# A two-layer diffusion trunk: kernel tiles of the state space loaded during the gates, modulation two row blocks a step

## The chip, the cores and the metric

The kernel runs on one core of one Trainium2 chip. The metric is the device time of one execution in microseconds (us); the time of a kernel is the median of its runs.

## What is computed

Two trunk layers over 256 context tokens and 256 latent tokens of width 1024, all in float32. Each layer computes, for both streams (the second layer for the latent one only, beyond k, v and u of the context):

```
mods = silu(c) @ ada_w + ada_b                         # 6 x 1024 per stream: shift, scale, gate, twice
h    = rmsnorm(x) * (1 + scale) + shift
q, k, v, u, g = split(h @ w_in)
o    = differential attention (two softmax maps a head, 4 heads of 64, axial rotary)
y    = u * d + sum over both directions of C x,  x_t = lam_bar x_(t-1) + b_bar u_t     # 32 groups of 16 channels, 64 states
y    = gelu(y);  y = y * sigmoid(y @ w_glu + b_glu)
x    = x + gate1 * rmsnorm((sigmoid(ga) * (o' @ w_br_a) + sigmoid(gs) * (y @ w_br_s)) @ w_out)
x    = x + gate2 * rmsnorm(squared-ReLU MLP(rmsnorm(x) * (1 + scale2) + shift2))
```

## The kernel before

**Order of the work.** The Python program emits one straight line of instructions; the framework's scheduler (line 1419, with a simulated timeline) then orders the instructions of each engine by the place in the program and by when it thinks that operands and buffers are ready. So an instruction may run well before or after its place in the text. All DMAs but one kind go out on SP's queue in the order that results.

**Weights.** A weight unit is 128 x 1024 floats, 512 KB. prefetch (line 188) loads it into a raw tile, ACT copies it to whi, DVE (for some units POOL) subtracts to get wlo, and each product is three matmuls (mm3, lines 158 to 161). Raw tiles come from a pool of five buffers (RW), whi and wlo from four each.

**Modulation.** ada_gen (line 279) is a background task: for each of eight row blocks of ada_w it loads a raw tile (two for part 0), from the same five buffers, and runs four small matmuls into one PSUM bank ("ada"); then it evacuates. Parts 1 to 4 of each layer have eight blocks each. The bank has one buffer, which ssm_out also uses.

**Background.** pump (line 675) runs the next step of the first task in a list, up to its next yield. The counts of pumps at each place are tables: in layer 0 three after each k unit (PK) and each v tile (PV), none in gates 0 to 7, one in each later gate (PG); in layer 1 three after each k unit, none at q and v, one in each gate. In layer 0 the list holds ssm_in, ssm_out and then parts 1 to 4; two pumps (FE) of the last tail of layer 0 and then layer 1 take parts 1 to 4 of layer 1.

**State space.** The sequence is cut into 32 chunks of 8 tokens. Inside a chunk the output is a product with a local kernel: ssm_out (line 530) computes for each of four chunks of eight groups, c = 0 to 3, the rows of CL (chunk state to output, stored to cl, 1 MB) and the local kernel, stored to kd. M is the local kernel in shifted copies: each of 128 partitions reads rows of 128 floats, 16 floats further for each of 8 shifts, so that the DMA moves runs of 512 bytes. ygen (line 1035) loads two M tiles of 1 MB and CL, and computes y by blocks b of groups from U and M, and from the scanned states S2 and CL (line 1073). Part of CL goes to the small pool (CLl, NX quarters of 512 KB), the rest to large slots (CLs).

**Buffers.** slot gives one of 15 large buffers (8 KB a partition), which hold nearly everything; xtile gives one of three small buffers (4 KB a partition), which also serve as scratch of the SSM steps (cm) and as x of the tails.

**Around the y products.** After q, k and v come 16 gate units (lines 1110 to 1122) with the items of the attention and, in layer 1, the scan between them. s2copy (after gate 15 in layer 0, after gate 10 in layer 1) makes S2. The y tasks start after gate 15 (YA). Then come the pa units (attention output by gate), gelu, glu and psb.

Of the kernel before, what the change touches and what calls it, by code (L numbers as in the profile page):

```python
# [68 lines left out]
YA = [15, 15]  # L69
YN = [2, 1]  # L70
UA = {2: 1, 3: 3}
NX = [4, 2]
LW = [1, 0]
HFA = [(3,), (0, 1, 2, 3), (), (1, 2, 3)]
HFQ = [(), (0, 1, 2, 3)]
# [10 lines left out]
def trunk(tc, I, out):  # L86
    nc = tc.nc
    ctx = ExitStack()
    with ctx:
# [189 lines left out]
        def ada_gen(L, g):  # L279


            c0, n = (0, 512) if g == 0 else (1024 + 1024 * g, 256)
            ncb = n // 128
            ps = pd_.tile([128, 512], F32, name="ada")
            for k in range(8):
                rows = I["ada_w"][L, k * 128:(k + 1) * 128]
                if (L, g) == (0, 0) and k < AK:
                    full = slot([2, 1024], name="adaw")
                    S.dma_start(out=full.rearrange("p j c -> p (j c)"), in_=rows[:, 0:2048])
                    raws = [full[:, 0], full[:, 1]]  # L290
                else:
                    raws = []
                    for jp in range(n // 256):
                        raw = rawp.tile([128, 1024], F32, name="raw", tag="raw")
                        S.dma_start(out=raw, in_=rows[:, c0 + jp * 1024:c0 + (jp + 1) * 1024])
                        raws.append(raw)
                for j in range(4):
                    raw, o = raws[j * n // 1024], j * n % 1024
                    PE.matmul(ps[32 * j:32 * j + 32, :n], cs[:, k, :], raw[:, o:o + n], start=(k == 0), stop=(k == 7))  # L299
                yield  # L300
            R = m2(n, name="row")
            if g in (1, 4):
                ab, gr = m2(n, name="ab"), m2(n, name="gr")
                S.dma_start(out=ab, in_=I["adab"][L, :, g // 4])
                S.dma_start(out=gr, in_=I["grow"][L, :, g // 4])
                V.tensor_tensor(R, ps[:, :n], ab, op=OP.add)
                V.tensor_tensor(R, R, gr, op=OP.mult)
                dd = dram.tile([2, 1024], F32, name=f"ggd{L}_{g}")
                for j in range(4):
                    S.dma_start(out=dd[:, j * n:(j + 1) * n], in_=R[32 * j:32 * j + 2])  # L310
                ggd[L, g] = dd
            else:
                A.activation(R[:, 0:n // 2], ps[:, 0:n // 2], AF.Copy)
                V.tensor_copy(R[:, n // 2:n], ps[:, n // 2:n])
                for cb in range(ncb):
                    PE.transpose(ps[:, cb * 128:(cb + 1) * 128], R[:, cb * 128:(cb + 1) * 128], ident)
                mt = perl.tile([128, 4, ncb, 2], F32, name=f"mod{g}")
                ptv = ps[:, :n].rearrange("p (cb j w) -> p j cb w", cb=ncb, j=4)[:, :, :, 0:2]

                def col(o, nj):  # L320
                    return vecs[L][:, o:o + ncb * nj].rearrange("p (j c) -> p j c", j=nj)[
                        :, :, :, None].to_broadcast([128, nj, ncb, 2])
                V.tensor_tensor(mt, ptv, col({0: V_AB, 2: V_SH2, 3: V_SC2}[g], 4), op=OP.add)
                if g == 0:
                    V.scalar_tensor_tensor(mt[:, 2:4], mt[:, 2:4], 1.0, col(V_G0, 2), op0=OP.add, op1=OP.mult)
                elif g == 3:
                    V.scalar_tensor_tensor(mt, mt, 1.0, col(V_G2, 4), op0=OP.add, op1=OP.mult)
                mods[L, g] = mt.rearrange("p j cb v -> p (j cb) v")
            yield
# [9 lines left out]
        ssmt = {}  # L339

        def ssm_params(L):
# [123 lines left out]
            ssmt[L]["b2"] = pcs[:, 640:1696].rearrange("p (r g h) -> p r g h", r=2, g=33)  # L465
            ssmt[L]["et"] = [dram.tile([128, 8, 2, 128], F32, name=f"et{L}_{c}") for c in range(4)]
            ssmt[L]["cl"] = [dram.tile([128, 8, 2, 128], F32, name=f"cl{L}_{c}") for c in range(4)]
            ssmt[L]["kd"] = [dram.tile([16, 16, 240], F32, name=f"kd{L}_{h}") for h in range(2)]
            yield

        def ssm_b(L):
# [58 lines left out]
        def ssm_out(L, c):  # L530

            z = ssmt[L]
            cch = z["bc"][:, 2:4, 8 * c:8 * c + 8]
            C = slot([8, 2, 128], name="CL")
            Cv = C.rearrange("p g r (s h) -> p g r s h", s=8)
            cmul(L, c, Cv[:, :, 0], cch[:, 0], cch[:, 1], OP.subtract)
            yield
            cmul(L, c, Cv[:, :, 1], cch[:, 1], cch[:, 0], OP.add)
            S.dma_start(out=z["cl"][c], in_=C)
            yield  # L540
            pks = [tbank("kf"), pd_.tile([128, 512], F32, name="ada")]
            b2f = z["b2"].rearrange("p r g h -> p r (g h)")
            for g2, r, j, d in np.ndindex(2, 2, 4, 2):
                ro, gi = slice(64 * d, 64 * d + 64), 4 * g2 + j
                PE.matmul(pks[d][32 * j:32 * j + 32, g2 * 128:(g2 + 1) * 128],
                          b2f[ro, r, (8 * c + gi) * 16:(8 * c + gi) * 16 + 32], C[ro, gi, r, :],
                          start=(r == 0), stop=(r == 1), tile_position=(64 * d, 32 * j))
            kt = chk.tile([128, 2, 240], F32, name="kt")
            pf, pb_ = (p[:, 0:256].rearrange("p (g n) -> p g n", g=2) for p in pks)
            V.tensor_copy(kt[:, :, 0:128], pb_)  # L550
            V.tensor_tensor(kt[:, :, 112:128], kt[:, :, 112:128], pf[:, :, 0:16], op=OP.add)
            for g2 in range(2):
                o = V_D + 2 * c + g2
                V.scalar_tensor_tensor(kt[:, g2, 112:128], eye16, vecs[L][:, o:o + 1], kt[:, g2, 112:128],
                                       op0=OP.mult, op1=OP.add)
            V.tensor_copy(kt[:, :, 128:240], pf[:, :, 16:128])
            for j in range(4):
                o = 8 * (c % 2) + j
                S.dma_start(out=z["kd"][c // 2][:, o:o + 5:4], in_=kt[32 * j:32 * j + 16])
            z["done", c] = True  # L560
            yield

# [201 lines left out]
        for L in range(DEPTH):  # L764
# [266 lines left out]


            ysb, yg, ygh, ygl = [], [], [], []

            def ygen():
                ysb.append(slot([4 // A_, 8, 2, 64], name="ysb"))
                Ms = {}
                while ("done", 3) not in z:
                    pump()
                for gh in range(2):  # L1040
                    M = slot([16, 128], name="M")
                    kd = z["kd"][gh]
                    S.dma_start(out=M.rearrange("p g n -> p (g n)"),
                                in_=bass.AP(tensor=kd.tensor, offset=kd.offset, ap=[[16, 8], [240, 256], [1, 128]]))
                    Ms[gh] = M
                CLs = {}
                for qd in range(8):
                    if qd < NX[L]:
                        t = xtile("CLl").rearrange("p (g r n) -> p g r n", g=4, r=2)
                        S.dma_start(out=t, in_=z["cl"][qd // 2][:, qd % 2 * 4:qd % 2 * 4 + 4])  # L1050
                        CLs[qd] = t
                    elif qd % 2 or qd == NX[L]:
                        if qd % 2 == 0:
                            t = slot([8, 2, 128], name="CLs")
                            S.dma_start(out=t, in_=z["cl"][qd // 2])
                            CLs[qd], CLs[qd + 1] = t[:, 0:4], t[:, 4:8]
                        elif qd not in CLs:
                            t = slot([4, 2, 128], name="CLs")
                            S.dma_start(out=t, in_=z["cl"][qd // 2][:, 4:8])
                            CLs[qd] = t  # L1060
                    elif qd not in CLs:
                        t = slot([8, 2, 128], name="CLs")
                        S.dma_start(out=t, in_=z["cl"][qd // 2])
                        CLs[qd], CLs[qd + 1] = t[:, 0:4], t[:, 4:8]
                for b in range(8 // A_):
                    ps = bbank("y")
                    for gi, r, a in np.ndindex(4, 3, A_):
                        g = b * 4 * A_ + 4 * a + gi
                        if r == 0:
                            w, mv = U[:, g, 64 - ncol:64], Ms[g // 16][:, g % 16]  # L1070
                        else:
                            w, mv = S2[g // 16][:, g % 16, r - 1], CLs[g // 4][:, g % 4, r - 1]
                        PE.matmul(ps[ncol * a:ncol * a + ncol, gi * 128:gi * 128 + 128], w, mv,
                                  start=(r == 0), stop=(r == 2), tile_position=(0, ncol * a))
                    A.activation(ysb[0][:, b // 2, :, b % 2].rearrange("p t (g h) -> p g t h", g=4),
# [34 lines left out]
            for j in range(16):  # L1110
# [3 lines left out]
                step(at, -(-nitem * (j + 1) // AJ[L]) - -(-nitem * j // AJ[L]))  # L1114
                step(sc, 8)
                pump(PG[L][j // 4])
                if j == SJ[L]:
                    s2copy()
                if j >= YA[L]:
# [311 lines left out]
```

## Time and profile before

| | us |
|---|---|
| median of 3 runs | 1327.86 |
| lowest, highest | 1326.23, 1328.57 |
| the profiled execution | 1329.41 |
| its span, first to last instruction | 1327.3 |
| TensorE busy in it | 1236.9 (93%) |
| VectorE (DVE) busy | 876.1 (66%) |
| ScalarE (ACT) busy | 535.1 (40%) |
| GpSimd (POOL) busy | 239.8 (18%) |
| mean granted TensorE clock | 0.977 of full speed |

PE is TensorE's matmuls, PEld its weight loads, SPq the queue of SP that issues DMAs. In a row of a timeline, the bracket holds the idle time of the engine before the instruction and what ended it. A wait for several things is put down to the one that came last. Records of a float32 matmul come in twos.

### The profile page before, as it was taken

The page shows a single profiled execution, that of the slowest core. Times are in us where ns is not written, and L with a number is a line of the kernel's source. Part 1 is how long each engine was busy: PE and PEld are TensorE (multiplying, and loading weights), DVE is VectorE, ACT ScalarE, POOL GpSimd, SP SyncE. Part 2 cuts the span into 40 slices and gives each one's busy share as a digit, 9 for nine tenths or more (in the row PEclk, how much of TensorE's full clock was granted, in tenths as well). Part 3 has the DMA queues.
Part 4 walks back from the last instruction along what each step waited for, and adds up shares of the span by engine and source line. Part 5 has one row for each costly group of instructions (what it writes and reads, how often), then busy time and mean ns, then how long its engine had stood idle before and what let it go on. Part 6 is the DMA issues. An engine that isn't in the chain of part 4 may idle for free.

```text
span 1327.3 us, 20706 instructions
## 1 busy us (share of the span) xinstructions
PE 1236.9 (93%) x8032; PEld 1000.1 (75%) x8032; DVE 876.1 (66%) x1786; ACT 535.1 (40%) x929; POOL 239.8 (18%) x284
## 2 busy tenths in 40 slices
PE   4699999997899999999999999989998889899997
PEld 1697767665777796677887888878776778799996
DVE  8779744433376764589978656844676757776666
ACT  1643345445343541222322223533453544544442
POOL 0001088500000330101201112611000001213122
PEclk9799999998999999999999999999999889999999
DMA  9353452216536355832454534368345786466562
GB/s 370 140 156 131 151 195 84 96 56 165 216 113 236 122 183 181 285 113 92 155 185 149 166 113 168 136 197 304 151 152 125 304 278 222 159 192 189 185 186 91
DMA packets 77043, 228.62 MB, mean 172 GB/s; under 512 B 15985, under 2 KB 26897, under 8 KB 72977
## 3 DMA queue, kind: packets, MB, share of 16 engines
q1 hardware_dynamic: 68624, 225.21, 50.5%
q10 hardware_dynamic: 8320, 2.10, 0.7%
q8 instruction: 63, 1.03, 0.3%
q14 instruction: 36, 0.29, 0.1%
HBM read 205.29 MB, written 21.99 MB: 171 GB/s over the span
## 4 chain that ended last, share of the span: by engine, by line
PE 77%; DVE 12%; DMA 5%; ACT 3%; issue 2%; POOL 1%; SPq 1%; DVEq 0%; ACTq 0%; POOLq 0%
PE m1p L159 6%; PE m1p L161 6%; PE m1p L160 6%; PE m2p L159 5%; PE m2p L160 5%; PE m2p L161 5%; PE ga L159 3%; PE ga L160 3%; PE ga L161 3%; PE ada L299 3%; PE S L917 3%; PE mo L159 2%; PE mo L160 2%; PE mo L161 2%; DMA raw<-in_wts 2%
## 5 line engine op out<-in xcount | busy, mean ns | idle before, releaser
L153 ACT ACTIVATE whi<-raw 128x1024 fp32r<-128x1024 f32 x208 | 219.6, 1060 | 381.0 <-PE m2p L161 97.1
L155 DVE TENSOR_TENSOR wlo<-raw,whi 128x1024 fp32r<-128x1024 f32 x200 | 248.0, 1242 | 127.8 <-ACT whi L153 125.3
L1252 POOL TENSOR_TENSOR zz<-zz 128x512 f32<-128x512 f32 (+1 forms) x64 | 88.7, 1386 | 414.9 <-ACT hid L1251 409.2
L159 PE MATMUL m1p<-h,whi 128*128 128x512 f32 (+1 forms) x448 | 151.7, 339 | 0.0
L161 PE MATMUL m1p<-h,wlo 128*128 128x512 f32 (+1 forms) x448 | 150.9, 337 | 0.0
L160 PE MATMUL m1p<-l,whi 128*128 128x512 f32 (+1 forms) x448 | 150.6, 336 | 0.0
L159 PE MATMUL m2p<-whi,hid 128*128 128x512 f32 x288 | 113.7, 395 | 0.2 <-DVE acc L1290 0.2
L160 PE MATMUL m2p<-wlo,hid 128*128 128x512 f32 x288 | 112.5, 391 | 0.0
L161 PE MATMUL m2p<-whi,hid 128*128 128x512 f32 x288 | 112.3, 390 | 0.0
L159 PEld LDWEIGHTS m1p<-h,whi 128*128 128x128 f32 x448 | 84.9, 189 | 13.1 <-issue 3.8
L160 PEld LDWEIGHTS m1p<-l,whi 128*128 128x128 f32 x448 | 84.9, 189 | 9.0
L161 PEld LDWEIGHTS m1p<-h,wlo 128*128 128x128 f32 x448 | 84.9, 189 | 9.0 <-issue 0.2
L159 PE MATMUL ga<-hh,whi 128*128 128x512 f32 (+1 forms) x256 | 89.4, 349 | 1.7 <-ACT whi L153 1.7
L161 PE MATMUL ga<-hh,wlo 128*128 128x512 f32 (+1 forms) x256 | 88.7, 346 | 0.0
L160 PE MATMUL ga<-hl,whi 128*128 128x512 f32 (+1 forms) x256 | 88.0, 344 | 0.0
L299 PE MATMUL ada<-raw,cs 128*32 128x256 f32 (+1 forms) x592 | 55.3, 422 | 13.7 <-DMA raw<-in_ada_w 13.7
L159 PEld LDWEIGHTS m2p<-whi,hid 128*128 128x128 f32 x288 | 54.0, 188 | 15.4 <-issue 2.5
L160 PEld LDWEIGHTS m2p<-wlo,hid 128*128 128x128 f32 x288 | 54.1, 188 | 12.4 <-issue 1.9
L161 PEld LDWEIGHTS m2p<-whi,hid 128*128 128x128 f32 x288 | 54.1, 188 | 11.0
L159 PEld LDWEIGHTS ga<-hh,whi 128*128 128x128 f32 x256 | 48.9, 191 | 15.4 <-issue 8.7
L1253 DVE TENSOR_TENSOR hid<-zz,hid 128x512 fp32r<-128x512 f32 (+1 forms) x64 | 37.9, 595 | 27.8 <-POOL zz L1252 27.5
L161 PEld LDWEIGHTS ga<-hh,wlo 128*128 128x128 f32 x256 | 49.0, 191 | 9.3 <-issue 4.1
(309 smaller groups left out, 2859.9 us busy)
## 6 DMA issues: line engine op xcount, KB each, us to landing
raw<-in_wts SPq DMA_DIRECT2D x227, 512.0 KB, 4.3
raw<-in_ada_w SPq DMA_DIRECT2D x84, 512.0 KB, 6.1
cl<-CL SPq DMA_DIRECT2D x8, 1024.0 KB
adaw<-in_ada_w SPq DMA_DIRECT2D x6, 1024.0 KB, 11.6
CLs<-cl SPq DMA_DIRECT2D x5, 1024.0 KB
x<-in_x SPq DMA_DIRECT2D x8, 512.0 KB, 4.6
M<-kd SPq DMA_DIRECT2D x4, 1024.0 KB
et<-ET SPq DMA_DIRECT2D x4, 1024.0 KB
```

What stands on the lines that cost most here:

```text
L153: a = A.activation(hi, src, AF.Copy)
L155: eng.tensor_tensor(lo, src, f(hi), op=OP.subtract)
L159: after(PE.matmul(ps, sh, mh, start=first, stop=False), prev)
L160: PE.matmul(ps, sh, ml, start=False, stop=False)
L161: PE.matmul(ps, sl, mh, start=False, stop=last)
L299: PE.matmul(ps[32 * j:32 * j + 32, :n], cs[:, k, :], raw[:, o:o + n], start=(k == 0), stop=(k == 7))
L917: PE.matmul(ps[:, :nk], qT[rr, h, qc:qc + 128], kT[rr, h, 0:nk], start=True, stop=True)
L1252: G.tensor_tensor(zz, zz, zz, op=OP.mult)
L1253: V.tensor_tensor(lo, zz, f(hi), op=OP.subtract)
```

## The change

Four edits that belong to two ideas. The local kernels are kept in DRAM by chunk (four tensors kd instead of two), and M becomes four tiles of 512 KB, each for one chunk of eight groups. Three of them come from the small pool, and their loads are placed at gates 11, 12 and 13 of layer 0 and 0, 4 and 8 of layer 1 (MJ). The fourth is loaded in ygen: before y block 1 into the small pool (layer 0), or after the second CLs load into a large slot (layer 1). CL now always goes to four large slots. And ada_gen, for parts 1 to 4, yields after every second row block, so that one pump does two of them.

```diff
-NX = [4, 2]
+MJ = [(11, 12, 13), (0, 4, 8)]
...
-                yield
+                if g == 0 or k % 2:
+                    yield
...
-            ssmt[L]["kd"] = [dram.tile([16, 16, 240], F32, name=f"kd{L}_{h}") for h in range(2)]
+            ssmt[L]["kd"] = [dram.tile([16, 8, 240], F32, name=f"kd{L}_{c}") for c in range(4)]
...
-                o = 8 * (c % 2) + j
-                S.dma_start(out=z["kd"][c // 2][:, o:o + 5:4], in_=kt[32 * j:32 * j + 16])
+                S.dma_start(out=z["kd"][c][:, j:j + 5:4], in_=kt[32 * j:32 * j + 16])
...
+            Ms = []
+
+            def mload():
+
+                while ("done", 3) not in z:
+                    pump()
+                q = len(Ms)
+                M = (slot([1024], name="M") if q == 3 and last else xtile("M"))
+                kd = z["kd"][q]
+                S.dma_start(out=M, in_=bass.AP(tensor=kd.tensor, offset=kd.offset, ap=[[16, 8], [240, 128], [1, 128]]))
+                Ms.append(M.rearrange("p (g n) -> p g n", g=8))
 
             def ygen():
                 ysb.append(slot([4 // A_, 8, 2, 64], name="ysb"))
-                Ms = {}
-                while ("done", 3) not in z:
-                    pump()
-                for gh in range(2):
-                    M = slot([16, 128], name="M")
-                    kd = z["kd"][gh]
-                    S.dma_start(out=M.rearrange("p g n -> p (g n)"),
-                                in_=bass.AP(tensor=kd.tensor, offset=kd.offset, ap=[[16, 8], [240, 256], [1, 128]]))
-                    Ms[gh] = M
-                CLs = {}
-                for qd in range(8):
-                    if qd < NX[L]:
-                        t = xtile("CLl").rearrange("p (g r n) -> p g r n", g=4, r=2)
-                        S.dma_start(out=t, in_=z["cl"][qd // 2][:, qd % 2 * 4:qd % 2 * 4 + 4])
-                        CLs[qd] = t
...
+                while len(Ms) < 3:
+                    mload()
+                CLs = []
+                for c in range(4):
+                    CLs.append(slot([8, 2, 128], name="CLs"))
+                    S.dma_start(out=CLs[c], in_=z["cl"][c])
+                    if c == 1 and last:
+                        mload()
                 for b in range(8 // A_):
+                    if b == 1 and not last:
+                        mload()
                     ps = bbank("y")
...
-                            w, mv = U[:, g, 64 - ncol:64], Ms[g // 16][:, g % 16]
+                            w, mv = U[:, g, 64 - ncol:64], Ms[g // 8][:, g % 8]
                         else:
-                            w, mv = S2[g // 16][:, g % 16, r - 1], CLs[g // 4][:, g % 4, r - 1]
+                            w, mv = S2[g // 16][:, g % 16, r - 1], CLs[g // 8][:, g % 8, r - 1]
...
                 pump(PG[L][j // 4])
+                if j in MJ[L]:
+                    mload()
```

## Rows read from the trace of the kernel before

**Rows 1.** The page: the chain that ended last, by engine

```profile
PE 77%; DVE 12%; DMA 5%; ACT 3%; issue 2%; POOL 1%; SPq 1%; DVEq 0%; ACTq 0%; POOLq 0%
```

**Rows 2.** Layer 0's y products: TensorE's timeline; slices (PE to POOL, PEclk, DMA, GB/s)

```profile
321.96 0.69 PE L1073 MATMUL y<-M,U 128*64 128x128 f32 x4 [6.33 <-DMA M<-kd]
...
332.73 0.44 PE L1073 MATMUL y<-M,U 128*64 128x128 f32 x4 [3.63 <-ACT on L949]
334.74 1.12 PE L1073 MATMUL y<-CLs,S 128*64 128x128 f32 x8 [1.57 <-DMA CLs<-cl]
...
322.00:324.00 2.00, 2.00 (x20) 2.00 (x22) 0.00 (x0) 0.00 (x0) 0.00 (x0) 0.50 0.62 116
334.00:336.00 2.00, 1.26 (x12) 1.26 (x14) 0.00 (x0) 0.00 (x0) 0.00 (x0) 0.58 0.98 406
```

**Rows 3.** Layer 1's late gates: SP's timeline, waits (total, times, longest), slices, DVE, loads

```profile
1007.60 7.83 SPq L1043 DMA_DIRECT2D M<-kd  x2
1016.22 7.80 SPq L204 DMA_DIRECT2D raw<-in_wts  x1
...
ACT whi L153 <- DMA raw<-in_wts: 23.3, 6, 14.7
DVE wlo L155 <- ACT whi L153: 20.0, 5, 11.4
...
PE ada L299 <- DMA raw<-in_ada_w: 11.2, 4, 9.5
...
PE glu L159 <- ACT ygh L1102: 3.4, 1, 3.4
...
1032.00:1034.00 2.00, 1.34 (x9) 0.53 (x10) 1.50 (x4) 1.75 (x5) 0.00 (x0) 0.50 1.05 430
1080.00:1084.00 4.00, 1.62 (x11) 0.79 (x11) 4.00 (x6) 1.46 (x3) 0.00 (x0) 0.73 0.82 278
...
L893 DVE TENSOR_TENSOR Vt<-Vt,s x62: 204/224/227, 944.4 to 1058.0; 128x64 f32<-128x64 f32 x62
...
L295 SPq DMA_DIRECT2D raw<-in_ada_w x11: 327/328/591, 1024.1 to 1079.0; - x11
```

**Rows 4.** Slices of a gate of layer 0, and of q and v of layer 1

```profile
220.00:230.00 10.00, 10.00 (x48) 6.98 (x48) 5.17 (x10) 5.11 (x12) 8.59 (x19) 1.00 0.17 52
930.00:940.00 10.00, 10.00 (x154) 8.30 (x153) 4.61 (x10) 4.46 (x10) 1.96 (x2) 1.00 0.93 385
940.00:950.00 10.00, 10.00 (x93) 6.70 (x91) 4.83 (x18) 3.44 (x8) 0.00 (x0) 1.00 0.01 2
```

**Rows 5.** DMA: SP's issues of M (ns, min/median/max); the page's row for weights (landing)

```profile
L1043 SPq DMA_DIRECT2D M<-kd x4: 625/2772/4967, 309.3 to 1010.6; - x4
...
raw<-in_wts SPq DMA_DIRECT2D x227, 512.0 KB, 4.3
```

**Rows 6.** Layer 0, end of v: ada loads on SP, TensorE's ada, the next weights

```profile
L295 SPq DMA_DIRECT2D raw<-in_ada_w x5: 328/328/356, 109.3 to 141.1; - x5
...
170.32 1.50 PE L299 MATMUL ada<-raw,cs 128*32 128x256 f32 x24
...
173.07 2.02 SPq L204 DMA_DIRECT2D raw<-in_wts  x4
```

**Rows 7.** The loads of CLl on SP; TensorE in layer 1's u stage

```profile
L1050 SPq DMA_DIRECT2D CLl<-cl x6: 319/374/648, 154.9 to 853.8; - x6
...
870.34 1.97 PE L659 MATMUL ht<-ident,xn 128*128 128x128 f32 x8 [4.40 <-DVE xn L653]
```

**Rows 8.** Layer 1, k and q: ada loads from 880 to 912 us, weights, q products

```profile
L295 SPq DMA_DIRECT2D raw<-in_ada_w x8: 328/328/421, 882.8 to 909.9; - x8
...
914.52 7.01 SPq L204 DMA_DIRECT2D raw<-in_wts  x6
...
L159 PE MATMUL q<-hh,whi x32: 278/283/384, 917.1 to 928.3; 128*128 128x256 f32 x32
```

More of the change, by code (lines that the diff above doesn't have):

```diff
@@ L1046, in ygen @@
-                CLs = {}
-                for qd in range(8):
-                    if qd < NX[L]:
-                        t = xtile("CLl").rearrange("p (g r n) -> p g r n", g=4, r=2)
-                        S.dma_start(out=t, in_=z["cl"][qd // 2][:, qd % 2 * 4:qd % 2 * 4 + 4])
-                        CLs[qd] = t
[L1052 to L1064, printed above, removed]
+                while len(Ms) < 3:
+                    mload()
```

## The prediction

> **What bounds the kernel now.** I read the page first: TensorE holds 77% of the chain that ended last [rows 1], so a loss is a hole in TensorE's work or a stretch at its lower clock. I then read the busy time in slices of 20 us. Apart from the start and the tails, two stretches stand out: 300 to 340 us, the local (y) products of layer 0, and 1020 to 1090 us, the end of layer 1's gates and its y products. I took both apart by the timeline of TensorE, by waits, by slices of 2 to 4 us and by what SP issues.
>
> In layer 0, TensorE stands 6.33 us until M lands, at 321.96, then 3.63 us (put down to ACT), then 1.57 us for CLs [rows 2]: 11.5 us. While M comes in, DMA moves 116 GB/s at a busy share of 0.62; in 334 to 336 us, with CLs and raw, 406 GB/s. The granted clock is 0.50 in 322 to 324 us, after the idle 6 us, and 0.58 in 334 to 336 us: the y products after a hole run at 1.2 GHz, not 2.4. This is so in about 322 to 328 and 334 to 338 us, some 9 us of work at 0.5 to 0.6, which costs about 4.1 us. The stage loses 15.6 us.
>
> In layer 1, SP takes 7.83 us over two M transfers from 1007.60, and 7.80 us over the weight load behind them, to 1024.02 [rows 3]. Only then can the ada load follow that TensorE waits for: 9.5 us. ACT stands 14.7 us at a weight split and DVE 11.4 us behind ACT. The clock is 0.50 in 1032 to 1034 us; with 4.6 us of work at it (to 1037 us) the hole costs 9.5 + 2.3 = 11.8 us. The scan, which y needs, runs on DVE until 1058.0 us and is late by DVE's 11.4. The backlog behind this costs more: TensorE works 1.62 of 4 us in 1080 to 1084 at a clock of 0.73, glu waits 3.4 us for gelu; with the smaller holes since 1050 us I count 9.7 us.
>
> **The change part by part.** *M loaded ahead.* Three of four M tiles, now 512 KB each, leave the y stage. At 116 GB/s one takes 0.52 MB / 116 GB/s = 4.5 us of DMA. The gates have room for it: the DMA share is 0.17 in 220 to 230 us [rows 4]. Layer 0: CLs takes the slots that M had; by 406 GB/s and the 4.3 us that a raw takes to land [rows 5], one issued at 309 us is there by about 315, as TensorE runs dry at 321.96 - 6.33 = 315.6. The y products of blocks 0 to 2 then cover the tail of the attention (o, its norm, ot, oh), which holds part of those 11.5 us: its steps on ACT and DVE get no shorter. I leave 4.6 us of holes; between none and all of the second and third waits (5.2) are possible. Gain 15.6 - 4.6 = 11.
>
> Layer 1: 11.8 us, since no M but the last is issued there. Of the 9.7 us of backlog I take 5: the 11 ada loads issued from 1024.1 to 1079.0 [rows 3] (5.8 MB, 13 us at 430 GB/s) go earlier, while CLs grows from 3 to 4 MB. Gain 17.
>
> *The fourth M* follows y block 0 (layer 0) or CLs 1 (layer 1): 4.5 us of DMA beside other work, pa units in layer 0. I cost it at nothing; without that cover it is 4.5 us each (see the rivals).
>
> *Two row blocks a step.* The matmuls are the same, 24 records or three blocks in 1.50 us [rows 6]; what moves is loads. A background step now takes two of the five raw buffers.
>
> (a) Layer 0, end of v: six steps there reach ada, so 6 blocks before, 10 now. Five ada loads, issued from 109.3 to 141.1, hold all five buffers until the bank they add into is free, at 170.3, and the gates' first weights leave at 173.07 [rows 6]. Four more blocks ahead of them cost 4 x 1.36 us (0.52 MB at 385 GB/s, the rate in 930 to 940 us [rows 4]) = 5.4 us by bandwidth, and 4 x 3.4 = 13.6 at the pace of (c); attention work covers some, so I put 4.
>
> (b) M needs no large slot any more. CLl, which comes from the same small pool and stands later in the program, was issued at 154.9 and 853.8 us [rows 7]; so M will leave about then too, and slowly. In layer 0 that is ahead of the gates' weights, 0 to 4.5 us: I take 2. In layer 1 it is beside the u weights, where TensorE waits 4.40 us for a norm anyway [rows 7]: 0 to 6 us, I take 2.
>
> (c) Layer 1, k: eight ada loads leave from 882.8 to 909.9 us [rows 8]. The steps at k now ask for 20 blocks instead of 11; with three done in the u stage, 17 are left. The third q weight, issued at 914.52, queues behind them. It is used at 917.1 + 2 x 2.9 = 922.9 and takes 4.3 us to land and 2.3 to be split, so it must leave by 916.3, or 920.8 with 9 blocks x 0.5 us more work on TensorE ahead of it. By bandwidth: 17 x 1.36 us + 6.8 MB of weights, U and ETl / 385 GB/s = 41 us from 882.8, or 924: a stall of 3. By the pace shown, 27.1 us / 8 = 3.4 us a block: 940.6, a stall of 20. I take 3, since nothing asked for more there before, and DMA is idle right after (2 GB/s in 940 to 950 us [rows 4]).
>
> (d) Layer 0's first tail has no background left to fill it with, two blocks of 0.5 us: 1.
>
> M is the only load that SP issues in another place; DMA bytes, kd writes and y products are the same in sum. Gains 11 + 17 = 28, costs 4 + 2 + 2 + 3 + 1 = 12, net 16. The profiled execution took 1329.41 us, 2.1 of it outside its span: 1313.4. The median of the runs lies 1.5 lower than that execution: **1312**.
>
> A rule to weigh: M's rows are 512 bytes, and the rows show 116 GB/s for it. The Trainium skill (DMA: Bandwidth & Descriptors, Specifications) gives 512 B as the size from which transfers run at line rate. By that M would take about a quarter of the time where it now goes, (b) would come to about 1 and the sum to 1309. The trace disagrees, so its rate is used.
>
> **The rivals.** *Both stages close up.* Holes of 2.6 us are left in layer 0 (gain 13), layer 1 gets 8 of the backlog (20), and the buffers cost 4: 1329.4 - 33 + 4 - 1.5 = 1299. For: fewer bytes at the end of layer 1. Against: the same five buffers for all loads.
>
> *The last M takes the place.* In layer 1 it goes out behind CLs 1 and blocks SP again, up to 4.97 us for one issue [rows 5], with CLs 2, 3 and the pa weights behind it. Price 4.5 + 5 there and 2 in layer 0: 1312 + 11.5, or 1323. For: it is on the path of y block 1. Against: it is half as long, and weights may be issued before it.
>
> *The raw buffers turn over no faster* (the slower side). The k stage keeps 3.4 us a block: 20 there, 13.6 in layer 0's first gates, 3 for the rest of the list, 36.6 against 28: 1329.4 + 8.6 - 1.5 = 1336. At p us a block it decides against the change where 17p - 38 + 4p + 3 > 28, from p = 3.0 on. For: one bank for all ada sums, whose hand-over from one part to the next holds every pair loaded. Against: few blocks were asked for at that pace.
>
> *M is still late*, because the small pool is taken: it also holds scratch of the SSM steps and x of the tails. CLl got through, so this has no chance of its own.
>
> **How the numbers follow.** Forecast, 1312 (own range 1304 to 1319): 0.50. Both close up, 1299: 0.13. Last M, 1323: 0.20, of which 0.04 ends within 0.2%. Buffers, 1336: 0.17, of which 0.02 within 0.2% and 0.15 above. About 0.2%, 2.7 us, is what a measurement of this kernel can tell from no change. Faster 0.79, same 0.06, slower 0.15. The range takes in the times of the first two rivals and ends short of the third, which leaves out some 0.2: 1298 to 1332.
>
> **What would show it.** Right: no wait for M at y in layer 0, y starting within 2 us of the gates' work; no SP issue over 2 us in layer 1's late gates, no idle of DVE over 3 us, no clock of 0.50 there. The costs: layer 0's first gate starting some 6 us later, M issued near 150 and 855 us, more ada loads in 880 to 930 us and q weights after them. Wrong: q or v of layer 1 standing for tens of us, or y of layer 1 waiting for M.

## The result, and the profile after

The runs of before here are those above and one more.

| | before | after |
|---|---|---|
| median of the runs, us | 1327.75 | 1306.99 |
| lowest, highest | 1326.23, 1328.57 | 1306.33, 1307.98 |
| ratio, 95% interval | | 0.9856 [0.9835, 0.9877] |
| span of the profiled execution | 1327.3 | 1305.3 |
| TensorE busy | 1236.9 | 1231.6 |
| the rest of the span | 90.4 | 73.7 |

The kernel is 20.8 us faster, where 16 were forecast. Of the 22.0 us of span, 16.7 are idle time of TensorE that went, and 5.3 are TensorE's own busy time.

The page's chain by engine, after (TensorE's share was 77% [rows 1]):

```profile
PE 79%; DVE 11%; DMA 4%; issue 2%; ACT 2%; POOL 1%; SPq 0%; DVEq 0%; ACTq 0%; POOLq 0%
```

Slices of after (us, busy time and instructions of PE, PEld, DVE, ACT, POOL, then the granted clock, DMA's busy share and GB/s):

```profile
320.00:340.00 20.00, 20.00 (x214) 14.93 (x207) 6.79 (x20) 9.08 (x25) 0.00 (x0) 1.00 1.02 361
322.00:324.00 2.00, 2.00 (x15) 1.76 (x13) 0.00 (x0) 0.00 (x0) 0.00 (x0) 1.00 0.98 414
...
1032.00:1034.00 2.00, 2.00 (x19) 2.00 (x19) 1.55 (x2) 2.00 (x3) 0.00 (x0) 1.00 0.96 395
1080.00:1084.00 4.00, 4.00 (x29) 3.71 (x29) 4.00 (x9) 4.00 (x7) 0.00 (x0) 1.00 0.53 161
...
180.00:185.00 5.00, 3.77 (x26) 1.85 (x22) 0.00 (x0) 0.84 (x3) 4.14 (x12) 0.50 1.03 405
980.00:990.00 10.00, 9.25 (x62) 7.34 (x60) 7.69 (x39) 2.85 (x13) 0.00 (x0) 1.00 0.00 1
1000.00:1010.00 10.00, 6.58 (x43) 5.26 (x44) 6.22 (x19) 5.02 (x9) 0.00 (x0) 0.83 0.85 320
```

The first four answer to [rows 2, 3]: TensorE is busy throughout and at full clock at the times of both bad stretches. The last three are new losses, one ahead of layer 0's first gate and two in layer 1's gates. SP's issues, after:

```profile
155.00 3.90 SPq L1043 DMA_DIRECT2D M<-kd  x2
...
170.72 0.62 SPq L1043 DMA_DIRECT2D M<-kd  x1
...
175.03 2.89 SPq L295 DMA_DIRECT2D raw<-in_ada_w  x5
...
180.38 3.83 SPq L204 DMA_DIRECT2D raw<-in_wts  x3
...
912.72 21.64 SPq L204 DMA_DIRECT2D raw<-in_wts  x10
...
1018.71 0.61 SPq L1043 DMA_DIRECT2D M<-kd  x1
1020.58 6.81 SPq L1053 DMA_DIRECT2D CLs<-cl  x1
```

M left from 155 us on, as forecast. The last M of layer 1 takes SP 0.61 us, where two took 7.83 before [rows 3]; but the CL load behind it takes 6.81 us, as the weight load behind M took 7.80 before, so M still holds SP, on the load that follows. TensorE shows no wait for it. The gates' first weights left at 180.38 instead of 173.07 [rows 6], behind five ada loads. Waits of after (total, times, longest), of TensorE in layer 1 and of SP at 968 to 1000 us:

```profile
PE u L159 <- ACT whi L153: 6.7, 3, 5.2
...
PE ga L159 <- ACT whi L153: 3.2, 1, 3.2
PE glu L159 <- ACT ygh L1095: 2.1, 1, 2.1
...
SPq L305 <- PE pdt L932: 21.3, 1, 21.3
```

The 21.3 us are new and were not forecast. The small bias load of modulation part 4 (line 305) waits for a buffer that the attention frees, and the gates' weights stand behind it in SP's queue: DMA is empty in 980 to 990 us. TensorE then works 6.58 of 10 us in 1000 to 1010, with 3.2 us of waits for the split of a gate weight. That SP stands is not a loss by itself. Before, it stood as long a little earlier in the layer, for the buffer of an ada load (waits of SP in 915 to 960 us):

```profile
SPq L295 <- DVE s L891: 22.8, 1, 22.8
```

TensorE stayed busy all the same (73.70 of 73.70 us from 887.6 to 961.3, and 38.70 of 38.70 to 1000).

**By stage.** The time between first matmuls of before and after shows more than the total. The windows below, of TensorE's ada instructions alone, have these ends: layer 0's first gate, its psb, the end of its MLP, layer 1's u end, first gate, and psb (us, busy time and instructions of PE and of PEld, clock, DMA share, GB/s). Before:

```profile
100.00:179.30 79.30, 3.21 (x48) 1.25 (x48) 1.00 0.43 144
179.30:385.90 206.60, 8.60 (x98) 3.08 (x98) 0.97 0.42 133
385.90:852.00 466.10, 19.40 (x175) 4.25 (x174) 1.00 0.47 159
852.00:887.60 35.60, 2.35 (x32) 0.73 (x32) 0.95 0.61 199
887.60:961.30 73.70, 4.71 (x72) 1.93 (x72) 1.00 0.64 232
961.30:1094.70 133.40, 13.78 (x152) 4.47 (x152) 0.94 0.66 215
```

After:

```profile
100.00:190.90 90.90, 7.32 (x80) 2.59 (x80) 0.93 0.48 160
190.90:381.00 190.10, 13.97 (x174) 4.74 (x174) 1.00 0.48 165
381.00:834.30 453.30, 9.81 (x68) 1.72 (x66) 1.00 0.43 148
834.30:872.30 38.00, 2.75 (x32) 0.94 (x32) 0.87 0.67 191
872.30:957.00 84.70, 11.54 (x160) 3.76 (x160) 1.00 0.75 267
957.00:1072.00 115.00, 4.49 (x64) 1.57 (x64) 0.97 0.57 200
```

The pairs carry modulation work from one stage to another, so each stage's change holds work that was moved. At 1.50 us for 24 records [rows 6] that is the fourth column, an estimate:

| stage | change, us | ada records | moved work | rest | M alone | pairs alone |
|---|---|---|---|---|---|---|
| to layer 0's first gate | +11.6 | +32 | +2.0 | +9.6 | +3.0 | +9.1 |
| its gates, y, pa | -16.5 | +76 | +4.8 | -21.3 | -16.0 | -1.2 |
| psb, MLP | -12.8 | -107 | -6.7 | -6.1 | -0.1 | -12.2 |
| layer 1, u | +2.4 | 0 | 0 | +2.4 | -1.5 | +1.7 |
| k, q, v | +11.0 | +88 | +5.5 | +5.5 | 0.0 | +10.7 |
| gates, y, pa | -18.4 | -88 | -5.5 | -12.9 | -13.9 | -7.9 |
| sum | -22.7 | +1 | +0.1 | -22.8 | -28.5 | +0.2 |

The last two columns are the stage changes (not the rest) of the first two experiments. The table is of one execution of each kernel. The place of a stage moves by up to 2 us between kernels that differ only behind it (layer 0's first gate: 179.3 in before and 177.5 in m_same, 190.9 in after and 189.0 in pk1, two of the experiments below), so entries of that size say little.

### The profile page after: what moved, and what is told of

Its sections match the earlier page's. It is cut to its first block, busy times and chain, and to the rows that moved or that the text cites. A ratio compares the mean times of both kernels' runs of the same rounds, so it can differ in the third digit from the quotient of the medians.

```text
span 1305.3 us, 20704 instructions
## 1 busy us (share of the span) xinstructions
PE 1231.6 (94%) x8032; PEld 998.3 (76%) x8032; DVE 873.5 (67%) x1786; ACT 534.8 (41%) x929; POOL 247.3 (19%) x284
## 4 chain that ended last, share of the span: by engine, by line
PE 79%; DVE 11%; DMA 4%; issue 2%; ACT 2%; POOL 1%; SPq 0%; DVEq 0%; ACTq 0%; POOLq 0%
PE m1p L159 6%; PE m1p L161 6%; PE m1p L160 6%; PE m2p L159 5%; PE m2p L161 5%; PE m2p L160 5%; PE ga L159 4%; PE ga L161 4%; PE ga L160 3%; PE mo L159 3%; PE mo L160 3%; PE mo L161 3%; PE S L917 3%; PE ada L299 3%; DVE wlo L155 2%
## 5 line engine op out<-in xcount | busy, mean ns | idle before, releaser
L1247 POOL TENSOR_TENSOR zz<-zz 128x512 f32<-128x512 f32 (+1 forms) x64 | 97.0, 1516 | 401.2 <-ACT hid L1246 400.5
L159 PEld LDWEIGHTS m2p<-whi,hid 128*128 128x128 f32 x288 | 54.0, 188 | 16.2 <-DVE acc L1285 2.6
L839 POOL TENSOR_TENSOR sh<-sh,rope 128x256 f32<-128x256 f32 x16 | 18.4, 1151 | 207.9 <-DVE sh L838 195.8
```

The lines of the kernel that those rows point to most:

```text
L159: after(PE.matmul(ps, sh, mh, start=first, stop=False), prev)
L839: G.tensor_tensor(sh, sh, rope[:, 1], op=OP.mult)
L1247: G.tensor_tensor(zz, zz, zz, op=OP.mult)
```

## The experiments

Each ratio stands against runs of the kernel before on the same chip.

### The two ideas apart

only_m is the changed kernel with one row block a step:

```diff
-                if g == 0 or k % 2:
-                    yield
+                yield
```

> The changed kernel with one row block a background step again: M early, nothing else. Theory (M is the gain, pairs only cost): no wait for M in layer 0's y products, no blocked SP at layer 1's late gates; the first gate of layer 0 starts by 183 us instead of 190.9, no stall at q of layer 1: 1295 to 1302 us. Rival (pairs are what empties layer 1's end): without them 11 ada loads come back after the gates of layer 1 and the stage from 1020 us loses 5 to 10 us again: 1308 to 1316 us.

Measured: 1302.89, ratio 0.9811 [0.9772, 0.9850], span 1299.4.

only_pairs is the kernel before with two row blocks a step:

```diff
-                yield
+                if g == 0 or k % 2:
+                    yield
```

> The kernel before with two row blocks a background step, M and CL as before. Theory: both M stalls stay (11.5 us of waits in layer 0, 9 to 12 us in layer 1) and the raw buffers cost at the gates of layer 0 (first gate at 185 to 191 us) and at k and q of layer 1: 1332 to 1342 us. Rival: the relief at layer 1's end outweighs this, 1318 to 1325 us.

Measured: 1331.11, ratio 1.0032 [1.0012, 1.0052], span 1327.9.

So the whole gain is M's: the pairs alone make the kernel 0.3% slower, and the median with M alone is 4 us below that with both (the intervals of these two ratios overlap). By medians the two ideas add up: -24.4 and +3.9 us alone, -20.8 together. With M alone the median is 0.9 us above the theory's range and well below its rival's, and layer 0's first gate starts at 182.3, as the theory said; for the pairs the theory's range lay a little high, with the first gate (188.4) inside it. The stall at line 305 is there with the pairs alone (22.2 us) and not with M alone. By the table above, M alone takes 16.0 and 13.9 us out of the two bad stretches and costs 3.0 ahead of layer 0's gates; in only_m the weights there leave earlier than in after, at 175.81:

```profile
175.19 0.58 SPq L295 DMA_DIRECT2D raw<-in_ada_w  x1
175.81 14.46 SPq L204 DMA_DIRECT2D raw<-in_wts  x9
```

### When M should leave

m_held is the changed kernel in which each M load is ordered behind the last weight load that prefetch issued before it:

```diff
-                S.dma_start(out=M, ...)
+                after(S.dma_start(out=M, ...), hold["w"])
```

> The changed kernel, but each M load is issued on SP only after the weight load that was last in the program before it, so that it can't run ahead of its gate. Theory: the loads that ran ahead cost 2 to 4 us in layer 0 (before the gates' first weights) and 2 to 6 us beside the u weights of layer 1; held, the first gate of layer 0 starts at 187 to 189 us, u of layer 1 waits less than 4 us, no new wait at y: 1301 to 1304 us. Rival (M ahead is free, the delay is the ada pairs' alone): first gate at 190 to 191 us and 1306 to 1310 us.

Measured: 1310.59, ratio 0.9862 [0.9820, 0.9905]. That can't be told from the changed kernel; the theory of a gain in the time falls, and the time of the rival, which gave none, fits better. The loads did move, from 155.0 to 252.8 us for the first and from 1018.7 to 1026.3 for the last:

```profile
L1043 SPq DMA_DIRECT2D M<-kd x8: 609/624/682, 252.8 to 1026.3; - x8
```

Layer 0's first gate comes 3.4 us earlier (187.5 against 190.9), as the theory said and the rival did not, but layer 1's gates end 4.7 later (1045.9 against 1041.2). M again leaves among the late weights there (996.1, 1007.8 and 1026.3 us), which fits but is not isolated by this run. So leaving early seems to cost in layer 0 and to pay in layer 1. The next kernel tests the first half.

only_m_held0 is only_m with the hold in layer 0 alone:

```diff
+                after(S.dma_start(out=M, ...), None if last else hold["w"])
```

> M early and one row block a step, with layer 0's M loads held behind the last weight load ahead of their gates; layer 1's M still free to run early. Theory (two costs that add in layer 0: pairs some 9 us, M ahead of the first gate weights some 3 us): first gate of layer 0 at 178 to 180 us against 182.3 without the hold, no new wait at y: 1298 to 1301 us. Rival (the 3 us are the kd stores' own): no change, 1301 to 1304 us.

Measured: **1297.23** (1295.54 to 1298.19), ratio 0.9780 [0.9754, 0.9806], the lowest median of all; it lies 9.8 us below the changed kernel and 5.7 below only_m (whose interval it overlaps). Its first gate starts at 178.1 (only_m: 182.3, before: 179.3), as the theory said; the time lies 0.8 us below the theory's range. The M loads now run from 226.9 to 997.6 us:

```profile
L1042 SPq DMA_DIRECT2D M<-kd x8: 599/620/710, 226.9 to 997.6; - x8
```

### Where the pairs cost

pv2 lets layer 0 pump twice instead of three times after each v tile; pk1 lets layer 1 pump once instead of three times after each k unit:

```diff
-PV = [3, 0]
+PV = [2, 0]
...
-PK = [3, 3]
+PK = [3, 1]
```

> The changed kernel with two instead of three background steps after each v tile of layer 0, so that 4 instead of 10 ada row blocks stand ahead of the gates' first weights (the others move to the gates). Theory (raw buffers full of ada pairs): first gate of layer 0 at 177 to 181 us instead of 190.9, 1296 to 1300 us. Rival (M and the kd stores on SP hold the weights): first gate at 187 to 191 us, 1305 to 1308 us.

> The changed kernel with one background step (two row blocks) instead of three after each k unit of layer 1, so that 8 instead of 20 row blocks are asked for there and the rest goes to the gates. Theory (the raw buffers at k delay the q weights): q follows k within 4 us, gates of layer 1 start at 947 to 951 us instead of 957.0; the later end of layer 1 loses part of that as the ada loads are back: 1300 to 1305 us. Rival (the longer k and q are only work moved forward): gates start early but the end comes back to 1306 to 1309 us.

Measured: pv2 1304.05, ratio 0.9819 [0.9775, 0.9862]; pk1 1299.30, ratio 0.9804 [0.9772, 0.9836].

With pv2 layer 0's first gate starts 13.4 us earlier (177.5), yet its psb only 8.8 earlier (372.2), and layer 1's u ends only 3.3 earlier (869.0). The blocks not done ahead of the gates are done later, so a late first gate costs about 3 us in the end, not 13. The median lies between the theory and its rival. With pk1 layer 1's first gate starts 14.9 us earlier (942.1 against 957.0) and 9.9 of it are left at psb (1062.1 against 1072.0): a little more than the theory gave. Of both, 2.3 us are there already when u ends (870.0 against 872.3), ahead of what the edit changes. Here the blocks asked for at k do cost, and the SP stall at line 305 is gone too; in pv2 it is still 21.3 us. The run does not separate the two. Since pk1 keeps the pairs and its median lies below that of only_m (1299.3 and 1302.9, with overlapping intervals), what costs there seems to be the number of blocks asked for at k, and not that they come in twos.

### Why M was slow

Up to here M's transfer rate, 116 GB/s [rows 2], was taken as given. The six kernels of this part keep M where it was before and change only what it reads, or where its rows lie. All but pitch read other numbers than the local kernel: they leave out the right y, and serve to time the load.

m_dense reads 8 KB in a row for each partition, m_512 reads 512 bytes at a time from a weight tensor, every run a different one:

```diff
-                    S.dma_start(out=M.rearrange("p g n -> p (g n)"),
-                                in_=bass.AP(tensor=kd.tensor, offset=kd.offset, ap=[[16, 8], [240, 256], [1, 128]]))
+                    S.dma_start(out=M, in_=z["cl"][gh].rearrange("p g r n -> p (g r) n"))
...
+                    wt = I["wts"][L, 16 * gh]
+                    S.dma_start(out=M, in_=bass.AP(tensor=wt.tensor, offset=wt.offset, ap=[[1024, 128], [131072, 16], [1, 128]]))
```

> The kernel before, its M loads at their old place and of the same size, but read from cl with 8 KB in a row for each partition instead of shifted rows of 512 bytes (so y is computed from other numbers). Theory (M's transfer rate is the cause of both stalls): the wait for M in layer 0 under 2 us instead of 6.3, SP issues M in under 2 us and no 7.8 us issue behind it in layer 1, DVE's wait for a split under 5 us instead of 11.4: 1305 to 1314 us. Rival (the place is the cause: two large tiles in the way of the weights): 1322 to 1328 us.

> The kernel before with M loaded at its old place as rows of 512 bytes, as there, but each byte once and the rows aligned (from the weights, so y is computed from other numbers). If the row length alone sets M's 116 GB/s: both stalls as before, 1324 to 1330 us, M at 110 to 130 GB/s. If the shifted, overlapping reads set it (rows of 512 bytes at line rate): as m_dense, 1305 to 1314 us, M over 250 GB/s.

Measured: m_dense 1303.17, ratio 0.9826 [0.9800, 0.9852]; m_512 1302.59, ratio 0.9821 [0.9795, 0.9848].

This is more than the theory gave, and as much as moving M brings (only_m 1302.89). With M in its old place and its old large slots, the time goes when M comes in fast. So the place costs only because of the rate, and the rate isn't the length of the run either: m_512 reads the same 512 bytes at a time as M. GB/s in 40 equal slices of 305 to 335 us, before and m_512 (M leaves at 309.3 and at 306.5):

```profile
GB/s 410 415 410 377 399 415 300 59 68 164 104 129 119 105 143 120 109 111 116 104 119 118 111 114 118 113 111 123 111 193 233 115 190 141 251 295 437 393 470 377
```

```profile
GB/s 366 399 361 224 158 278 298 314 230 223 326 342 340 341 382 427 415 415 437 415 404 404 437 404 410 421 426 437 404 393 410 410 131 55 22 0 0 0 0 0
```

The stretch at 104 to 143 GB/s in before, some 16 us for two tiles of 1 MB, is M; in m_512 as many bytes go mostly at 220 to 340 and are through by about 315 us.

What else is odd in M's read: neighbouring partitions start 64 bytes apart, the outermost of its three steps has a count of 8, and the rows of kd lie 960 bytes apart. One kernel for each:

```diff
m_shift
+                    ap=[[16, 128], [240 * 128, 16], [1, 128]]
...
m_outer8
+                    ap=[[262144, 8], [1024, 256], [1, 128]]
...
pitch (reads kd itself)
-            ssmt[L]["kd"] = [dram.tile([16, 16, 240], F32, name=f"kd{L}_{h}") for h in range(2)]
+            ssmt[L]["kd"] = [dram.tile([16, 16, 256], F32, name=f"kd{L}_{h}") for h in range(2)]
...
-                                in_=bass.AP(tensor=kd.tensor, offset=kd.offset, ap=[[16, 8], [240, 256], [1, 128]]))
+                                in_=bass.AP(tensor=kd.tensor, offset=kd.offset, ap=[[16, 8], [256, 256], [1, 128]]))
```

> As m_512 (the kernel before, M at its old place, read from the weights), but the 128 partitions read rows of 512 bytes that start 64 bytes apart and overlap, as M's do; the outermost step of the access still counts 128. If the shift and the overlap slow M: 110 to 150 GB/s while it comes in, 1318 to 1330 us. If the outermost step of 8 does (m_outer8): as m_512, 1300 to 1306 us.

> As m_512 (aligned rows of 512 bytes, each byte once, from the weights), but the access has 8 as its outermost step, as M's has, and 256 rows below it. If an outermost step of 8 leaves half of the DMA engines idle: 110 to 220 GB/s while it comes in, 1315 to 1330 us. If the shift and overlap are what counts: as m_512, 1300 to 1306 us.

> The kernel before with one thing changed: the rows of kd in DRAM lie 1024 bytes apart instead of 960 (240 floats and 16 unused). M's place, size, row length, shift and overlap and the order of the instructions are as before. If the distance of 960 bytes between the rows that follow each other makes M slow (all else was tried: row length, shift with overlap, outermost step): M at 250 to 310 GB/s, both stalls gone, 1300 to 1308 us. If it is something else of kd (that it is written in the kernel, or that the whole tile is read eight times from 245 KB): 110 to 130 GB/s and 1325 to 1330 us.

Measured: m_shift 1303.48, ratio 0.9815 [0.9751, 0.9880]; m_outer8 1302.31, ratio 0.9806 [0.9736, 0.9877]; pitch 1326.67, ratio 1.0001 [0.9981, 1.0020].

None of the three is the cause: the first two are as fast as m_512 although each has one of M's oddities, and pitch is as slow as before although it lacks one. Nor is it that few bytes are read many times over: by their access patterns a tile of m_shift reads 138 KB nearly eight times, one of M 245 KB about four times. What is left is that M's eight groups of 16 partitions read the same 256 rows, 64 bytes apart. m_same differs from m_outer8 in one number, the outermost step, and reads the same input tensor:

```diff
-                    ap=[[262144, 8], [1024, 256], [1, 128]]
+                    ap=[[16, 8], [1024, 256], [1, 128]]
```

> As m_outer8 (M at its old place in the kernel before, read from the weights, outermost step of 8), with that step 64 bytes instead of 1 MB: as in M, eight groups of 16 partitions read the same 256 rows at the same time, each 64 bytes further on. The rows lie 4096 bytes apart in an input, not 960 in kd. If DMA engines that read the same rows together slow each other: 110 to 190 GB/s, 1315 to 1330 us. If it is kd itself (written in the kernel, small): over 250 GB/s, 1300 to 1306 us.

Measured: 1326.38, ratio 0.9987 [0.9967, 1.0007], as slow as before. GB/s in the slices of 305 to 335 us, of m_same and m_outer8:

```profile
GB/s 366 328 393 399 208 104 93 141 123 114 91 158 173 140 143 106 109 107 91 99 89 98 143 158 157 182 195 236 228 216 308 382 470 393 431 421 399 410 421 431
```

```profile
GB/s 421 317 355 415 350 106 315 347 348 346 346 350 345 354 480 415 426 426 415 437 355 437 410 426 437 388 431 415 431 410 388 421 197 55 0 0 0 0 0 0
```

And SP's issues of m_same, where the second M and the CL load behind it block SP as in before:

```profile
307.50 8.74 SPq L1044 DMA_DIRECT2D M<-in_wts  x2
316.42 7.11 SPq L1055 DMA_DIRECT2D CLs<-cl  x1
```

With the eight groups on the same rows the transfer runs at some 90 to 180 GB/s; with the eight on different rows, at 315 to 354. That one number of the access is the cause of the slow rate in m_same, and as m_same has about M's rate and the time of before, it is taken as the cause for M. What inside the memory or the DMA engines makes it so no run shows, nor how the rate depends on the number of groups or on their distance. A kernel that keeps eight copies of kd, so that each group has rows of its own, was not tried; nor was pk1 together with only_m_held0.

## Why the prediction was right, and where it wasn't

The time lay in the range, on the faster side, and the first part of the mechanism is shown: two stretches lost time to M, and without it there they mostly close. The terms, as the prediction put them:

| term | forecast | measured |
|---|---|---|
| layer 0's y stage | -11 | -16.5 |
| layer 1's late gates | -17 | -18.4 |
| (a) and (b), layer 0's first gate | +4, +2 | +11.6 |
| (b), layer 1's u | +2 | +2.4 |
| (c), layer 1's k | +3 | +11.0 |
| (d), rest of layer 0 | +1 | -12.8 |
| from layer 1's psb on | 0 | +0.7 |
| sum | -16 | -22.0 |

**Layer 0's y stage** was mis-sized. The prediction named all 15.6 us [rows 2] and left 4.6 of them as holes, because the tail of the attention gets no shorter. It got its cover: in after TensorE is busy 20.00 of 20 us there, and M alone gives 16.0. Over the whole stage TensorE stood 16.2 us before (busy 190.45 of 206.60) and not at all after (190.10 of 190.10), with 76 more ada records in it.

**Layer 1's gates** came out as summed, but not as split. M alone gives 13.9 where the hole was put at 11.8. The other 4.5 are less than the work that the pairs carried off (5.5 by record count, 8.8 by ada's own busy time, 13.32 in only_m and 4.49 here), so some was lost again; the stall at line 305 may be that (no run isolates it). The prediction booked the lighter load here as a gain and booked the same blocks nowhere else as a cost.

**(a) and (b) in layer 0**: 3.0 from M and 9.1 from the pairs alone, against 2 and 4. Of 11.6, 2.0 are moved work. TensorE shows much of the rest as waits for an ada load and for the evacuation that frees the bank, at the lower clock (0.50 in 180 to 185 us):

```profile
179.24 1.08 PE L299 MATMUL ada<-raw,cs 128*32 128x256 f32 x8 [3.59 <-DMA raw<-in_ada_w]
...
186.53 1.93 PE L299 MATMUL ada<-raw,cs 128*32 128x256 f32 x16 [2.77 <-DVE row L307]
```

The price of (a) lies within its bounds (up to 13.6), but at more than twice the 4 that was put; pv2 shows that most of it is given back.

**(b) in layer 1**: right in size, wrong in cause. M alone costs nothing in the u stage (-1.5), so M did lie beside other work. The 2.4 us come with the pairs (1.7 alone): TensorE's waits for the split of a u weight are 0.2 us before, 2.3 in only_m, 5.7 in only_pairs and 6.7 in after.

**(c)**: the stage grew by 11.0. Of this 5.5 are moved blocks (6.8 by ada's own busy time), which the prediction used to find when the third weight is due and then left out of the sum. TensorE's idle time in the stage is 3.4 us, and none before: the stall itself was forecast at 3. The pace of 3.4 us a block, on which the slower rival rested, did not return.

**(d)** has the wrong sign, and is the largest error. Fewer background blocks in layer 0's tail and MLP is first of all less work: 107 records fewer, 6.7 us at the pace of blocks in a row, 9.6 by ada's own busy time in the two windows (19.40 and 9.81), as a record there takes 0.11 us (19.40 / 175) and in a run of three blocks 0.06. Of the rest, 0.4 is idle time and 2.8 busy time of the other products, of which there are as many; why those take less is open.

Work that moves was thus counted at its old place in one stage and at its new place in none. By stage the moves are +2.0, +4.8, -6.7, +5.5 and -5.5, which add to 0.1: they make the stages come out wrong and leave the sum alone. Without them (the column of the rest) the stages still miss the forecast, by +3.6, -10.3, -7.1, +0.4, +2.5 and +4.1, which add to -6.8. That errors of both signs left the time within 5 us of the forecast is in part luck. By idea the prediction did better: it has M at -18.8 (11 + 11.8 less 2 and 2) and the pairs at +3 (4 + 3 + 1 less the 5 of backlog), and the medians of each alone gave -24.4 and +3.9. M was put too small, mostly in layer 0's y stage.

Some of its signs did not come. In layer 1's late gates SP took over 2 us for a load (the 6.81 of the CL load, not the last M), and DVE waited up to 3.5 us for a split, where at most 3 was named (11.4 before).

**The rivals.** Both stages gave about what the first said (34.9 us against 33), but its price for the costs, 4 us, was too low. The last M did hold SP through the CL load behind it (6.81 us, the order of the 5 that this rival put), but TensorE had no wait for CL or M at y, so the price of 4.5 + 5 us was not paid. The buffers turned over fast enough. None of the rivals asked for the kernel without the pairs, which is at 1302.9.

**The rule that was weighed.** The prediction set M's 116 GB/s against the Trainium skill (DMA: Bandwidth & Descriptors, Specifications), which gives 512 B as the size from which transfers run at line rate, and said that the trace disagrees. It doesn't: at the same 512 B, m_outer8 moves 315 to 354 GB/s and m_512 mostly 220 to 340, beside other loads. Using M's own rate was right for M as it stands; taking it as a matter of the run's length was not, and it hid the question that mattered, why M is slow at all.

## What to carry to other kernels

Where a transfer runs at a quarter of the rate of its neighbours, ask first why, before giving it more time or another place: here a different source address, in kernels that only time the load, was worth as much as moving it (1302.6 and 1302.9). When background work is regrouped, book every block twice, out of its old stage and into its new one; only the stalls are then gain or loss. Look at what stands in the queue behind a load that must wait for a buffer: one bias load kept SP from issuing for 21.3 us with gate weights behind it, and a gate weight was then late, while a stand of 22.8 us before cost nothing.

## What the runs showed of the hardware that was not expected

A DMA whose eight groups of 16 partitions read the same rows, 64 bytes apart, ran at about 90 to 180 GB/s, from an internal tensor and from an input alike, and with rows 960, 1024 or 4096 bytes apart (before, pitch, m_same). The same shape with the groups on different rows ran at 315 to 354 (m_outer8), and 128 partitions that start 64 bytes apart in 16 separate regions at 290 to 353 (m_shift, 312 to 317 us). SP was held by the slow transfer too, and again on the load behind it: it took 8.74 us to issue two such M loads and 7.11 for the CL load behind them, against 3.04 and 0.49 in m_outer8.
